# Two sums and two low halves of every moving side on GpSimd in place of VectorE

## The chip, the cores and the metric

One core of a Trainium2 chip runs the whole kernel. The metric is the device time of one execution in microseconds (us). The engines are named as in the profile: PE is TensorE (matmuls), DVE is VectorE, ACT is ScalarE, POOL is GpSimd, SP is the engine that issues most of the loads.

## The reference, cut to what matters

Two transformer blocks in fp32 on a sequence of 2048 tokens of width 1024. The first mixes tokens (a pooling, a differential attention and a stick-breaking attention) and ends in a gated feed-forward layer; the second has a modulated norm, a gated MLP over chunks and a retention, an output projection and a gated residual.

```python
def first_block(x, ...):
    h = rmsnorm(x, norm1_g[l]); p = einsum('bsd,de->bse', h, w_in[l])
    ...
    x = x + einsum('bse,ed->bsd', concat([pool, diff, stick]), w_out[l])
    h2 = rmsnorm(x, norm2_g[l])
    gate = jnp.einsum('bsd,df->bsf', h2, w_gate[l])
    up = jnp.einsum('bsd,df->bsf', h2, w_up[l])
    x = x + jnp.einsum('bsf,fd->bsd', jax.nn.silu(gate) * up, w_down[l])
    return rmsnorm(x, final_norm_g)

def hybrid_layer(x, c, ...):           # the second block
    h = rmsnorm_2(x, g_pre) * (1.0 + scale[:, None, :]) + shift[:, None, :]
    proj = jnp.einsum('bsd,de->bse', h, w_in)
    ...
    y = rmsnorm_2(jnp.einsum('bsm,md->bsd', y, w_out), g_post)
    return x + gate[:, None, :] * y
```

The dense products of the feed-forward layer (width 2816) and of the second block's projections are the ones that this case is about.

## The kernel before, in words

**Products.** Every fp32 matmul is made of three products of halves: an operand `x` is split into a high half, which ScalarE writes (`split`, the copy L133), and a low half, the difference, which VectorE writes (L134); high·high, high·low and low·high are added up in PSUM. The dense layers add a scheme with seven products in place of eight on 2x2 blocks (`seven`, products L1025). Its left operands (stationary, tiles `l` and the sums `sf` of L1001) change with every step; its right operands (moving, tiles `r`) stay for a whole group of steps, and are built by `moving`.

**A moving side.** It has seven parts, named 11, t1, t2, t3, 21, 22 and t4, each with one buffer of its own: the blocks 11, 21 and 22 themselves and four sums: t1 = 11 − 12 (L949), t2 and t3 = 22 less what stands in the buffers (L980), and t4 = 21 less t2's source (L949 again, with the argument `a`; below it is called the fourth sum). The sources are loaded in pieces of 128x1024 into the pool `stg` of five buffers (L937, issued by SP); block 22 is loaded twice, once for L980 and once for its own split. Each part has two pieces, so a part takes two high halves on ScalarE and two low halves on VectorE. A step's products use the parts in the order 11, t1, t2, t3, 21, 22, t4.

**Where they are built.** Eight times a moving side is replaced while products go on: twice for the hidden layer (`hidden_moving`), three times for the way down (`down_moving`, groups of 6, 8 and 8 blocks of the hidden width; in the first group the second piece is 128x512), and three times in the second block (`second_moving`). A part can be written as soon as the last product with the old part is through, so at such a seam the building runs between the last steps of the old side and the first of the new one. The parts of a ninth moving side, at the very start (`first=True`), are built in another order.

**Order.** The program is written as above, and a scheduler with priorities (`high_priority`) sets the order on each engine; each engine then works strictly in its order. Other names: `wk` and `acc` are work tiles and PSUM banks of the products, with the additions L1042, L1044, L1132, L1137 and L1199 that read PSUM on VectorE; L1031 copies the first product; L1129 and L1189 are output transfers that GpSimd issues; L1403 to L1406 are the rotary embedding of the second block, of which L1404 runs on GpSimd or VectorE; L1624 to L1628 the group norm of the retention, with small operations L180 and L182 on GpSimd; L814 an addition of the attention stage on GpSimd.

Of the kernel before, what the change touches and what calls it, by code (L numbers as in the profile page):

```python
# [9 lines left out]
F32 = mybir.dt.float32  # L10
# [3 lines left out]
ALU = mybir.AluOpType  # L14
# [96 lines left out]
class Body:  # L111
# [15 lines left out]
        return self.tc.high_priority(self.pri[kind])  # L127


    def split(self, hi, lo, src):  # L130

        nc = self.nc
        nc.scalar.activation(hi, src, AF.Copy)  # L133
        nc.vector.tensor_tensor(out=lo, in0=src, in1=hi.bitcast(F32), op=ALU.subtract)  # L134

    def wgroup(self, w, k0, nk, c0, ncols):

# [804 lines left out]
    def moving(self, get, nk, first=False):  # L942

        nc = self.nc
        pieces = [(c, min(2, nk - c)) for c in range(0, nk, 2)]

        def less(out, x, y, engine=nc.vector):
            for (c, n), o, u, v in zip(pieces, out, x, y):
                engine.tensor_tensor(out=o[:, :n], in0=u[:, :n], in1=v[:, :n], op=ALU.subtract)  # L949

        def part(name, src):
            t = self.t(self.rp[name], [P, 2, 4, TB], "r", F32R, align=512)
            for (c, n), u in zip(pieces, src):
                self.split(t[:, 0, c:c + n], t[:, 1, c:c + n], u[:, :n])
            return t
        r = {}
        if first:
            r11, r21 = get(0, 0), get(1, 0)
            r["11"] = part("11", r11)
            r["21"] = part("21", r21)  # L960
            r12, r22 = get(0, 1), get(1, 1)
            r["22"] = part("22", r22)
            less(r11, r12, r11)
            r["t1"] = part("t1", r11)
            less(r11, r22, r11)
            r["t2"] = part("t2", r11)
            less(r12, r22, r12)
            r["t3"] = part("t3", r12)
            less(r11, r21, r11)
            r["t4"] = part("t4", r11)  # L970
            return r
        a = get(0, 0)
        r["11"] = part("11", a)
        b = get(0, 1)
        less(a, b, a)
        r["t1"] = part("t1", a)
        for p in range(len(pieces)):
            (c, n), u = pieces[p], get(1, 1, p)[0]
            for o in (a[p], b[p]):
                nc.vector.tensor_tensor(out=o[:, :n], in0=u[:, :n], in1=o[:, :n], op=ALU.subtract)  # L980
        r["t2"] = part("t2", a)
        r["t3"] = part("t3", b)
        r21 = get(1, 0)
        r["21"] = part("21", r21)
        less(a, r21, a)
        r["22"] = part("22", get(1, 1))
        r["t4"] = part("t4", a)
        return r

# [717 lines left out]
```

## Time and profile before

| what | value |
|---|---|
| median of 3 runs | 3583.6 us (3579.54 to 3586.99) |
| profiled execution, its own time | 3589.32 us |
| its span | 3587.6 us |
| PE busy | 3373.3 us, 94% |
| DVE busy | 2485.1 us, 69% |
| ACT busy | 1638.3 us, 46% |
| POOL busy | 932.3 us, 26% |
| products L1025 | 8400 matmuls, 1962.9 us busy, 66.6 us idle before them |

Busy shares are means over the whole span, whose stages differ. The profiled execution is one of several; the span is what the trace covers, and the execution's own time is 1.7 us more.

### The profile page before, as it was taken

The page shows a single profiled execution, that of the slowest core. Times are in us where ns is not written, and L with a number is a line of the kernel's source. Part 1 is how long each engine was busy: PE and PEld are TensorE (multiplying, and loading weights), DVE is VectorE, ACT ScalarE, POOL GpSimd, SP SyncE. Part 2 cuts the span into 40 slices and gives each one's busy share as a digit, 9 for nine tenths or more (in the row PEclk, how much of TensorE's full clock was granted, in tenths as well). Part 3 has the DMA queues.
Part 4 walks back from the last instruction along what each step waited for, and adds up shares of the span by engine and source line. Part 5 has one row for each costly group of instructions (what it writes and reads, how often), then busy time and mean ns, then how long its engine had stood idle before and what let it go on. Part 6 is the DMA issues. An engine that isn't in the chain of part 4 may idle for free. (4 is left out here: it accounts for less than half of the span.)

```text
span 3587.6 us, 47292 instructions
## 1 busy us (share of the span) xinstructions
PE 3373.3 (94%) x16504; PEld 2790.7 (78%) x16504; DVE 2485.1 (69%) x4265; ACT 1638.3 (46%) x3160; POOL 932.3 (26%) x1328
## 2 busy tenths in 40 slices
PE   7989989998879999999999999989999999999989
PEld 5777868886667877888878888778777878788867
DVE  8566674768888857666696667676759887433586
ACT  5347574647676644333343334333556544222243
POOL 3222243314652111111000000211233343333222
PEclk9999999999989999999999999999999999999999
DMA  5367655555533544333263233765786632422353
GB/s 171 123 201 239 182 155 183 172 162 164 173 110 108 159 138 145 116 106 106 85 217 124 91 122 97 154 156 113 170 211 205 206 112 96 146 86 89 112 177 133
DMA packets 458158, 521.51 MB, mean 145 GB/s; under 512 B 43088, under 2 KB 326400, under 8 KB 457920
## 3 DMA queue, kind: packets, MB, share of 16 engines
q1 hardware_dynamic: 401536, 358.26, 33.6%
q0 software_dynamic: 56384, 160.24, 15.0%
q8 instruction: 130, 2.13, 0.2%
q14 instruction: 108, 0.88, 0.1%
HBM read 360.55 MB, written 157.84 MB: 144 GB/s over the span
## 5 line engine op out<-in xcount | busy, mean ns | idle before, releaser
L1025 PE MATMUL acc<-r,l 128*128 128x512 f32 x8400 | 1962.9, 394 | 66.6 <-ACT r L133 20.4
L1025 PEld LDWEIGHTS acc<-r,l 128*128 128x128 f32 x8400 | 1585.4, 190 | 417.3 <-ACT r L133 29.3
L133 ACT ACTIVATE l<-sf 128x512 fp32r<-128x512 f32 (+1 forms) x408 | 251.9, 623 | 550.6 <-PE acc L1025 352.0
L133 ACT ACTIVATE l<-raw 128x512 fp32r<-128x512 f32 (+1 forms) x306 | 189.8, 622 | 423.2 <-PE acc L1025 406.5
L134 DVE TENSOR_TENSOR l<-sf,l 128x512 fp32r<-128x512 f32 (+1 forms) x408 | 280.7, 689 | 73.0 <-ACT l L133 70.8
L679 PE MATMUL s<-k,q 128*128 128x512 f32 (+2 forms) x960 | 272.1, 393 | 30.9 <-DMA q<-qkd 7.1
L134 DVE TENSOR_TENSOR l<-raw,l 128x512 fp32r<-128x512 f32 (+1 forms) x306 | 208.8, 687 | 125.9 <-ACT l L133 125.6
L679 PEld LDWEIGHTS s<-k,q 128*128 128x128 f32 x960 | 166.3, 197 | 68.4 <-DVE s L710 14.6
L1129 POOL DMA_DIRECT2D act<-wk x88 | 48.7, 553 | 621.8 <-DVE wk L1128 613.9
L806 DVE TENSOR_TENSOR_SCAN s<-s,one 128x512 f32<-128x512 f32 (+3 forms) x160 | 187.4, 1203 | 22.3 <-ACT s L802 15.7
L1001 DVE TENSOR_TENSOR sf<-raw 128x512 f32<-128x512 f32 (+1 forms) x102 | 74.5, 731 | 177.2 <-DMA raw<-act 89.3
L717 ACT ACTIVATE s<-s,mx 128x128 f32<-128x128 f32 (+15 forms) x128 | 154.3, 1206 | 84.7 <-DVE mx L713 82.5
L133 ACT ACTIVATE r<-stg 128x1024 fp32r<-128x1024 f32 (+1 forms) x120 | 120.5, 1028 | 123.7 <-PE d L162 23.6
L1189 POOL DMA_DIRECT2D x<-wk x96 | 83.3, 886 | 321.3 <-DVE wk L1199 225.0
L160 PE MATMUL d<-ws,h 128*128 128x512 f32 (+1 forms) x384 | 153.4, 402 | 0.7 <-DVE h L213 0.7
L738 PE MATMUL o<-v,pT 128*128 128x128 f32 x1088 | 149.2, 277 | 4.9 <-ACT pT L746 4.5
L738 PEld LDWEIGHTS o<-v,pT 128*128 128x128 f32 x1088 | 140.7, 192 | 15.5 <-ACT pT L746 8.2
L162 PE MATMUL d<-ws,h 128*128 128x512 f32 (+1 forms) x384 | 146.9, 385 | 0.0
L161 PE MATMUL d<-ws,h 128*128 128x512 f32 (+1 forms) x384 | 146.7, 384 | 0.0
L814 POOL TENSOR_TENSOR s<-s,s 128x1024 f32<-128x1024 f32 x48 | 123.8, 2579 | 73.1 <-DVE s L806 47.1
L134 DVE TENSOR_TENSOR r<-stg,r 128x1024 fp32r<-128x1024 f32 (+1 forms) x120 | 140.6, 1188 | 2.9 <-ACT r L133 2.8
L134 DVE TENSOR_TENSOR ws<-raw,ws 128x1024 fp32r<-128x1024 f32 x72 | 95.4, 1328 | 53.4 <-ACT ws L133 52.8
(322 smaller groups left out, 5777.5 us busy)
## 6 DMA issues: line engine op xcount, KB each, us to landing
raw<-in_w_in_dram SPq DMA_DIRECT2D x72, 512.0 KB, 4.6
k<-qkd SPq DMA_DIRECT2D x120, 256.0 KB, 4.3
q<-qkd SPq DMA_DIRECT2D x96, 256.0 KB, 4.6
x<-wk POOLq DMA_DIRECT2D x96, 256.0 KB, 5.7
raw<-in_w_gate_dram SPq DMA_DIRECT2D x44, 512.0 KB, 4.0
raw<-in_w_up_dram SPq DMA_DIRECT2D x44, 512.0 KB, 3.9
act<-wk POOLq DMA_DIRECT2D x88, 256.0 KB, 3.0
v<-vd SPq DMA_DIRECT2D x80, 256.0 KB, 3.2
```

The source lines that it names most:

```text
L133: nc.scalar.activation(hi, src, AF.Copy)
L134: nc.vector.tensor_tensor(out=lo, in0=src, in1=hi.bitcast(F32), op=ALU.subtract)
L160: self.nc.tensor.matmul(ps, st(0), mv(0), start=i == 0, stop=False)
L161: self.nc.tensor.matmul(ps, st(0), mv(1), start=False, stop=False)
L162: self.nc.tensor.matmul(ps, st(1), mv(0), start=False, stop=i == n - 1)
L679: nc.tensor.matmul(ps[:, :w], q[:, hl, c * P:(c + 1) * P], kt[:, o:o + w], start=hl == 0, stop=hl == 1 and not extra)
L717: nc.scalar.activation(e[:, :nk], e[:, :nk], AF.Exp, scale=-1.0, bias=mx[:, m, np_ - 1:np_], accum_out=s1[:, c, m:m + 1])
L738: nc.tensor.matmul(ops[:, c * P:(c + 1) * P], pT[:, j * P:(j + 1) * P], vs[kt // NT][:, kt % NT], start=kt == 0, stop=kt == nt - 1)
L806: nc.vector.tensor_tensor_scan(out=omb[:, c, :w][:, ::-1], data0=omb[:, c, :w][:, ::-1], data1=self.one.to_broadcast([P, w]), initial=1.0 ...
L814: nc.gpsimd.tensor_tensor(out=beta[:, two], in0=beta[:, two], in1=omb[:, two, 1:w + 1], op=ALU.mult)
L1025: nc.tensor.matmul(ps, l[lk][:, a, k], r[rk][:, b, k], start=first and k == 0 and i == 0, stop=k == nk - 1 and i == 2, skip_group_check=no ...
L1189: nc.gpsimd.dma_start(out=self.x1_d[b][row + i * P:row + (i + 1) * P, j * TB:(j + 1) * TB], in_=t, accum_op=ALU.add)
```

## The change

In the eight moving sides that are built while products go on, the fourth sum (both pieces) and the low halves of block 22 (both pieces) are computed by GpSimd in place of VectorE. The operations, their shapes and their operands stay the same.

```diff
-    def split(self, hi, lo, src):
+    def split(self, hi, lo, src, engine=None):
 
         nc = self.nc
         nc.scalar.activation(hi, src, AF.Copy)
-        nc.vector.tensor_tensor(out=lo, in0=src, in1=hi.bitcast(F32), op=ALU.subtract)
+        (engine or nc.vector).tensor_tensor(out=lo, in0=src, in1=hi.bitcast(F32), op=ALU.subtract)
...
-        def part(name, src):
+        def part(name, src, engine=nc.vector):
             t = self.t(self.rp[name], [P, 2, 4, TB], "r", F32R, align=512)
             for (c, n), u in zip(pieces, src):
-                self.split(t[:, 0, c:c + n], t[:, 1, c:c + n], u[:, :n])
+                self.split(t[:, 0, c:c + n], t[:, 1, c:c + n], u[:, :n], engine)
...
         r["21"] = part("21", r21)
-        less(a, r21, a)
-        r["22"] = part("22", get(1, 1))
+        less(a, r21, a, nc.gpsimd)
+        r["22"] = part("22", get(1, 1), nc.gpsimd)
         r["t4"] = part("t4", a)
```

The scheduler sets new orders. At the second seam (from 1786 us, the second half of the tokens in the hidden layer) GpSimd's rows read as follows. The tiles are: stg_16998 and stg_17000 (last number of the name) the two pieces of the fourth sum, stg_17036 and stg_17038 block 21, stg_17047 and stg_17049 block 22, r_17051 part 22.

```order
 L1129 DMA act2_0_99<-wk_3898_16823 128x512
+L949 TENSOR_TENSOR stg_3925_16998<-stg_3935_17036,stg_3925_16998 128x1024
 L1129 DMA act2_0_99<-wk_3924_16979 128x512
+L949 TENSOR_TENSOR stg_3926_17000<-stg_3936_17038,stg_3926_17000 128x1024
+L134 TENSOR_TENSOR r_3940_17051<-stg_3938_17047,r_3940_17051 128x1024
 L1129 DMA act2_0_99<-wk_3922_16963 128x512
+L134 TENSOR_TENSOR r_3940_17051<-stg_3939_17049,r_3940_17051 128x1024
```

The four new rows stand between the issues of three output transfers, which GpSimd did alone here before.

On VectorE at the same place (part t2 is r_17026, t3 r_17031, 21 r_17040, t4 r_17056) the rows before were:

```order
L134 TENSOR_TENSOR r_3933_17026<-stg_3926_17000,r_3933_17026 128x1024
L949 TENSOR_TENSOR stg_3925_16998<-stg_3935_17036,stg_3925_16998 128x1024
L134 TENSOR_TENSOR r_3934_17031<-stg_3929_17009,r_3934_17031 128x1024
L1001 TENSOR_TENSOR sf_3947_17073<-sf_3945_17068,raw2_3942_17061 128x512
L1001 TENSOR_TENSOR sf_3949_17078<-raw2_3942_17061,raw2_3943_17063 128x512
L134 TENSOR_TENSOR r_3937_17040<-stg_3936_17038,r_3937_17040 128x1024
L134 TENSOR_TENSOR l_3946_17070<-sf_3945_17068,l_3946_17070 128x512
L1128 TENSOR_TENSOR wk_3922_16963<-wk_3922_16963,wk_3918_16932 128x512
L949 TENSOR_TENSOR stg_3926_17000<-stg_3936_17038,stg_3926_17000 128x1024
```

In the new order the two rows of L949 are gone from this stretch, and so are part 22's two rows some places later; the rest of it stands in the same order, and t4's first low half has moved up into the place behind it.

On ScalarE at the fourth seam (from 2338 us, the second group of the way down; t3 is r_21337, 21 r_21346, 22 r_21357, t4 r_21362):

```order
 L133 ACTIVATE r_4721_21332<-stg_4714_21306 128x1024
+L133 ACTIVATE r_4729_21362<-stg_4713_21304 128x1024
 L133 ACTIVATE r_4722_21337<-stg_4717_21315 128x1024
-L133 ACTIVATE r_4729_21362<-stg_4713_21304 128x1024
 L133 ACTIVATE r_4725_21346<-stg_4724_21344 128x1024
 L133 ACTIVATE r_4728_21357<-stg_4726_21353 128x1024
+L133 ACTIVATE r_4729_21362<-stg_4714_21306 128x1024
 L133 ACTIVATE l_4736_21381<-sf_4735_21379 128x512
 L133 ACTIVATE r_4728_21357<-stg_4727_21355 128x1024
 L133 ACTIVATE l_4738_21386<-sf_4737_21384 128x512
-L133 ACTIVATE r_4729_21362<-stg_4714_21306 128x1024
```

Both high halves of t4 have moved up, the first ahead of t3's second piece.

## Rows read from the trace of the kernel before

**Rows 1.** Waits of PE over the whole run: us in total, times, longest.

```profile
PE acc L1025 <- ACT r L133: 20.4, 19, 2.3
...
PE acc L1025 <- DVE r L134: 8.3, 10, 1.7
```

**Rows 2.** Windows of eight seams: us, busy PE, PEld, DVE, ACT, POOL, clock, DMA.

```profile
2217.00:2248.00 31.00, 29.96 (x131) 24.16 (x130) 30.92 (x49) 17.89 (x30) 1.66 (x3) 1.00 0.52 157
...
sum 325.00, PE 276.94 PEld 217.06 DVE 314.64 ACT 168.62 POOL 43.97; mean PE 34.62 PEld 27.13 DVE 39.33 ACT 21.08 POOL 5.50
```

**Rows 3.** Lines L949 and L814: duration ns least/median/most, first and last start.

```profile
L949 DVE TENSOR_TENSOR stg<-stg,stg x32: 685/1219/1234, 1303.4 to 3415.3; 128x1024 f32<-128x1024 f32 x30, 128x512 f32<-128x512 f32 x2
...
L814 POOL TENSOR_TENSOR s<-s,s x48: 2162/2282/3187, 501.0 to 1114.7; 128x1024 f32<-128x1024 f32 x48
```

**Rows 4.** Timeline at 2839.5: start us, duration us, engine, line, tiles, shapes.

```profile
2839.82 0.68 DVE L1001 TENSOR_TENSOR sf<-sf,raw 128x512 f32<-128x512 f32 x1
2839.99 1.66 POOL L1404 TENSOR_TENSOR wk<-wk,rot 128x512 f32<-128x512 f32 x1 [6.02 <-DVE wk L1383]
2840.42 1.78 DVE L1001 TENSOR_TENSOR sf<-raw,raw 128x512 f32<-128x512 f32 x1
```

**Rows 5.** Timeline at 2884 to 2899, within S7.

```profile
2886.59 11.37 POOL L1404 TENSOR_TENSOR wk<-wk,rot 128x512 f32<-128x512 f32 x1 [1.63 <-DVE wk L1383]
...
2897.99 0.42 DVE L1405 TENSOR_TENSOR wk<-wk,wk 128x256 f32<-128x256 f32 x1 [1.19 <-POOL wk L1404]
```

**Rows 6.** Timeline of S2, 1805 to 1822: part of DVE and PE.

```profile
1805.80 1.23 DVE L134 TENSOR_TENSOR r<-stg,r 128x1024 fp32r<-128x1024 f32 x1
...
1810.48 1.23 DVE L134 TENSOR_TENSOR r<-stg,r 128x1024 fp32r<-128x1024 f32 x1
...
1811.61 1.23 DVE L949 TENSOR_TENSOR stg<-stg,stg 128x1024 f32<-128x1024 f32 x1
...
1814.03 1.42 PE L1025 MATMUL acc<-r,l 128*128 128x512 f32 x5 [0.72 <-DVE r L134]
...
1815.08 1.23 DVE L134 TENSOR_TENSOR r<-stg,r 128x1024 fp32r<-128x1024 f32 x1
...
1816.37 5.81 PE L1025 MATMUL acc<-r,l 128*128 128x512 f32 x24 [0.92 <-DVE r L134]
```

**Rows 7.** Timelines of S1, S4 and S6: PE where it idled.

```profile
1390.34 1.88 PE L1025 MATMUL acc<-r,l 128*128 128x512 f32 x7 [0.31 <-DVE r L134]
...
2368.32 5.41 PE L1025 MATMUL acc<-r,l 128*128 128x512 f32 x16 [0.52 <-DVE r L134]
...
2714.36 1.43 PE L1025 MATMUL acc<-r,l 128*128 128x512 f32 x5 [0.92 <-DVE r L134]
...
2720.38 1.88 PE L1025 MATMUL acc<-r,l 128*128 128x512 f32 x7 [1.93 <-ACT r L133]
```

**Rows 8.** Timeline of S5, 2522 to 2541; SP's row from its own timeline.

```profile
2524.60 1.23 DVE L134 TENSOR_TENSOR r<-stg,r 128x1024 fp32r<-128x1024 f32 x1 [1.89 <-ACT r L133]
...
2529.62 1.22 DVE L949 TENSOR_TENSOR stg<-stg,stg 128x1024 f32<-128x1024 f32 x1
...
2530.90 1.47 SPq L937 DMA_DIRECT2D stg<-in_w_down_dram  x2
...
2535.95 5.28 PE L1025 MATMUL acc<-r,l 128*128 128x512 f32 x22 [2.28 <-ACT r L133]
```

**Rows 9.** Timeline of S7, 2874 to 2892.

```profile
2880.49 2.35 DVE L980 TENSOR_TENSOR stg<-stg,stg 128x1024 f32<-128x1024 f32 x2
...
2889.30 2.93 PE L1025 MATMUL acc<-r,l 128*128 128x512 f32 x6 [4.64 <-ACT wk L1031]
```

**Rows 10.** Timeline of S8, 3414 to 3430.

```profile
3417.98 1.07 POOL L1624 TENSOR_TENSOR vq<-rn_m,c_ret_qdec 128x4 f32<-128x4 f32 x1 [5.58 <-DVE rn_m L1476]
...
3422.47 1.11 DVE L1628 TENSOR_SCALAR tmp<-tmp,rn_m,vq 128x128 f32<-128x128 f32 x4 [1.20 <-POOL vq L1626]
...
3424.97 5.18 PE L1025 MATMUL acc<-r,l 128*128 128x512 f32 x12 [3.82 <-DVE l L134]
```

## Prediction

> **What bounds the kernel now.** I read the page first: TensorE is busy almost throughout, and the question is where it is not. The view of TensorE's waits [rows 1] names, among others, the two operations that build a moving side: products L1025 waited 20.4 us for the high halves (ScalarE, L133) and 8.3 us for the low halves (VectorE, L134) of tiles `r`. The timeline then puts nearly all of that at eight places, the seams at which the stationary weights change and a new moving side must be built: S1 at 1366–1400 us, S2 1786–1832, S3 2217–2248, S4 2338–2382, S5 2505–2547, S6 2685–2732, S7 2861–2906, S8 3389–3425. The third view, busy time in these windows [rows 2], shows who is short there: VectorE worked 314.64 of 325.00 us, ScalarE 168.62, GpSimd 43.97. TensorE lacks 325.00 − 276.94 = 48 us in them. So VectorE is the bound of the seams, GpSimd looks free, and outside them neither matters. The reader is to see why one would move rows from VectorE to GpSimd, and then ask whether the two can work at the same time.
>
> **The change part by part.** Per seam four instructions go from VectorE to GpSimd: two L949 (the fourth sum, t4's source) and two L134 (low halves of block 22). That is 8 × 4 = 32, of which 30 are 128x1024 and 2 are 128x512; nothing else is added, no bytes and no product.
>
> *What a row costs on each side.* On VectorE a 128x1024 row takes 1.22 us [rows 3], and consecutive rows start about 1.14 us apart (1811.61 less 1810.48 is 1.13, [rows 6]); the 32 rows are about 31 × 1.14 = 35 us of VectorE's time. On GpSimd I find a subtraction or addition of this shape only in the attention stage: L814, 2.16 us at least and 2.28 in the median [rows 3]. I take 2.16, since the least is the one that waited for nobody.
>
> *Whether they overlap.* This decides. In [rows 4] VectorE ran the same L1001 shape twice: 0.68 us, and then 1.78 us for the row that began at 2840.42, when GpSimd's L1404 (from 2839.99 to 2841.65) was running; the second ended 0.55 us after L1404's end, as if it had been held and then done. In [rows 5] it is the other way round: GpSimd's L1404, the same shape that took 1.66, took 11.37 us from 2886.59 while VectorE went from row to row, and it ended at 2897.96, in VectorE's next gap (1.19 us idle, released by that very L1404). So a GpSimd row and a VectorE row with both inputs in SBUF take turns. GpSimd's turn holds VectorE for 2.16 us, and each moved row gives VectorE 1.14 and can take 2.16: a loss of 1.02 rather than a gain of 1.14. Over 32 rows that is about 33 us of VectorE time more in place of 35 less.
>
> The Trainium skill, "SBUF — State Buffer", section "SBUF: two separate sides", states this as a rule: VectorE and GpSimd share a port pair under an exclusive lock, which a VectorE instruction with two SBUF inputs or a GpSimd instruction takes for its whole length, whichever starts first, and the other blocks fully. By that rule moving work between the two gains nothing while both have work; the trace agrees (1.78 beside 0.68, and 11.37 beside 1.66), and shows besides that a dense row of VectorE instructions can keep GpSimd out for 11 us. With the rule the sum is the one worked out below; without it, each engine at its own pace, the 35 us of relief would lead to the third rival's time.
>
> *What of it lies on TensorE's path.* Only rows that TensorE waits for within the seam count; the moved rows themselves are needed late (22 and t4 are the last products of a step), and the 24 matmuls from 1816.37 on run in one piece [rows 6], so what VectorE is relieved of there is worth nothing.
>
> S2, worked in full [rows 6]. TensorE idles 0.72 before 1814.03 and 0.92 before 1816.37, both times for a low half; the second of these halves, begun on VectorE at 1815.08, ended at 1816.31, 0.06 before TensorE went on: no slack. In the new order both sums stand on GpSimd. The first has its operands at 1807.03 (VectorE's split of the tile at 1805.80 is through), before these rows; the second has them when the row of 1810.48 is through. Each can hold VectorE for 2.16, and one removed L949 (1811.61) gives back 1.14. With both holds the row of 1815.08 is 2 × 2.16 − 1.14 = 3.2 us late, with one 1.0; TensorE follows it. I take 2.6, nearer to the upper end, as both sums are ready while VectorE is full.
>
> S1, S4, S6 have the same build, and again rows that end when TensorE waits for them [rows 7]: 0.31, 0.52 and 0.92 us idle behind DVE r L134. Bounds as in S2, 1.0 to 3.2; middle 2.1 each, 6.3 together. In S4 the order of ScalarE moves too: t4's first high half, which waits for GpSimd's sum, now stands ahead of t3's second.
>
> S5 may gain. There the sum L949 at 2529.62 sets free the staging buffer into which the first piece of block 22 is loaded: the load is issued on SP's queue at 2530.90, and TensorE idles 2.28 until 2535.95 for the high half that ScalarE makes of it [rows 8]. VectorE had a gap of 1.89 us before 2524.60, with the sum's operands there at its end; GpSimd can run it then, and the load goes out about 4 us earlier. At best that takes away 2.28; at worst the same holds as elsewhere cost 1.0. I take −1.5.
>
> S7: the pair L980 at 2880.49 reads the buffer into which the next piece is loaded, so the load goes out behind it, and TensorE idles 4.64 until 2889.30 at the end of that chain [rows 9]. The first sum's operand is ready at 2880.5, so GpSimd can step in between the two: 0 to 2.16, I take +1.5. S8: TensorE idles 3.82 behind a chain of small GpSimd instructions, L1624 at 3417.98 to the multiply L1628 at 3422.47 that waits for it [rows 10]; the last moved row stands within this chain in GpSimd's order: 0 to 2.2, I take +1.1. In S3 TensorE works 29.96 of 31.00 us [rows 2], so little waits: 0 to 1.0, I take +0.3.
>
> Sum: 2.6 + 6.3 − 1.5 + 1.5 + 1.1 + 0.3 = **+10.3 us**. The bounds together: 1.0 + 3.0 − 2.3 + 0 + 0 + 0 = +1.7, and 3.2 + 9.6 + 1.0 + 2.2 + 2.2 + 1.0 = +19.2. The profiled execution took 3589.3 us, 5.7 above the median of 3583.6, so I expect about 3599.6 for a profiled execution like it and **3594** for the median.
>
> **The rivals.**
> *Shut out.* GpSimd does not step in but waits, as in [rows 5], some 10 us behind VectorE's rows. Then VectorE is not held at first, but t4's sum is late; ScalarE and VectorE, which work in order, then stand before t4's halves with other splits behind them. A seam in which that happens loses 5 to 10 us in place of 1 to 3. For it: the 11.37. Against: VectorE has gaps as soon as it lacks an input, and L1404 of [rows 4] did get in at once. In two to four seams it makes +15 to +30: **3599 to 3614**, middle 3606.
>
> *Nothing to see.* The holds fall into time that VectorE has to spare, for it is given 1.14 us a row back too; the late rows are made up before TensorE reads them. This needs most of the terms at their lower bound: −3 to +6, **3581 to 3590**. Against it stand the rows without slack at S2 and [rows 7].
>
> *Faster.* If GpSimd works beside VectorE without holding it, or gets its turns only in VectorE's gaps, the earlier loads and lighter VectorE are all gain: 2.28 in S5, the same kind of wait in S6, where a L949 also stands before a load (1.93 idle at 2720.38, [rows 7]), the waits for low halves 1.14 in S2, 0.52 in S4, 0.31 in S1, and 1.1 in S8, where one row less stands before the chain: 7.3 us, **3576**. It decides from the point where a seam's four rows cost VectorE less than the 4.6 us that they give it: fewer than about two held turns a seam. [Rows 4] speak against it.
>
> **How the numbers follow.** The forecast (held turns, some seams slower by 1 to 3 us) has 0.52, shut out 0.14, nothing to see 0.22, faster 0.12. About 0.2%, 7.2 us, is what a measurement of this kernel tells from no change. Slower by more than that, above 3590.8: four fifths of the forecast's own cases (0.42), all of the first rival (0.14), a little of the second (0.04): 0.60. Faster, below 3576.4: some two thirds of the third: 0.09. Same: the rest, 0.31. The likeliest case's own range is 3585 to 3603. For 8 in 10 I go up into the first rival, to 3610, and down to 3580, through most of the second.
>
> **What would show it.** Right: moved rows on GpSimd of 2.2 us and more in the seams, VectorE rows of 3.3 us beside them (1.22 + 2.16 less what had passed), TensorE's wait for `DVE r L134` in S2, S4 and S6 up by 1 to 3 us each from 8.3 in all [rows 1], its wait at 2535.95 in S5 shorter. Wrong: VectorE rows that stay at 1.22 beside GpSimd's (no turns), or GpSimd rows of 10 us (the first rival), or a TensorE whose waits in the seams are those of before. What would make the number wrong though the turns are right: the scheduler's new order on ScalarE, whose effect I have put at nothing but for S4.

## The result, and the profile after

The changed kernel takes 3613.2 us (median of 4 runs, 3608.1 to 3617.3) where the kernel before takes 3583.4 (4 runs): 29.8 us more, ratio 1.0083 (95% interval 1.0065 to 1.0100). Slower was forecast, and the reason given for it is what the trace shows; but the sum of +10 was a third of it, and 3613 lies above the range. The profiled execution took 3608.1 us, its span 3606.1. The spans of the two profiled executions differ by 18.5 us only: the one before took 8.5 us longer to reach S1, a stretch that the change does not touch, so the two traces are compared seam by seam here.

The moved rows themselves and two of the groups beside them, by line (duration ns least/median/most, first and last start; here as in the later fences of this view):

```profile
L949 POOL TENSOR_TENSOR stg<-stg,stg x16: 1736/3290/7330, 1367.0 to 3426.3; 128x1024 f32<-128x1024 f32 x15, 128x512 f32<-128x512 f32 x1
...
L134 POOL TENSOR_TENSOR r<-stg,r x16: 1612/2855/3403, 1382.8 to 3436.8; 128x1024 fp32r<-128x1024 f32 x15, 128x512 fp32r<-128x512 f32 x1
...
L134 DVE TENSOR_TENSOR r<-stg,r x104: 678/1214/3421, 18.7 to 3435.6; 128x1024 fp32r<-128x1024 f32 x98, 128x512 fp32r<-128x512 f32 x6
...
L1001 DVE TENSOR_TENSOR sf<-sf,raw x102: 549/683/2892, 15.6 to 3563.7; 128x512 f32<-128x512 f32 x94, 128x384 f32<-128x384 f32 x8
```

A row that took 1.22 us on VectorE [rows 3] takes 3.29 and 2.86 us on GpSimd in the median, up to 7.33. And VectorE's rows of the same lines, which before never exceeded 1.24 (`r<-stg,r`) and 0.71 (`sf<-sf,raw`), now reach 3.42 and 2.89, which is the usual row and 2.2 us on top. Counted over the trace from 1340 us on, VectorE has 50 additions and subtractions that are over 0.3 us longer than the usual row of their size, 73.6 us too long together; before there were 19 with 16.2. So 31 rows more are held, for 57 us: 29 of the 32 moved rows run beside such a long row.

TensorE's waits over the whole run, the answer to [rows 1]:

```profile
PE acc L1025 <- ACT r L133: 22.0, 16, 2.6
...
PE acc L1025 <- DVE r L134: 14.4, 11, 3.3
...
PE acc L1025 <- DVE wk L1042: 6.2, 3, 3.8
...
PE acc L1025 <- POOL r L134: 3.5, 2, 3.1
```

The wait for low halves from VectorE rose from 8.3 to 14.4; new are waits for VectorE's PSUM additions (L1042, 0.3 us before), and for GpSimd's own rows.

S2 in the timeline, beside [rows 6]:

```profile
1801.79 5.05 POOL L949 TENSOR_TENSOR stg<-stg,stg 128x1024 f32<-128x1024 f32 x1 [20.13 <-DVE r L134]
...
1805.12 3.94 DVE L134 TENSOR_TENSOR r<-stg,r 128x1024 fp32r<-128x1024 f32 x2
...
1807.97 2.58 PE L1025 MATMUL acc<-r,l 128*128 128x512 f32 x10 [0.85 <-DVE r L134]
1808.06 3.24 POOL L949 TENSOR_TENSOR stg<-stg,stg 128x1024 f32<-128x1024 f32 x1 [0.72 <-issue]
1808.98 2.87 DVE L1001 TENSOR_TENSOR sf<-sf,raw 128x512 f32<-128x512 f32 x1
...
1811.41 1.06 ACT L133 ACTIVATE r<-stg 128x1024 fp32r<-128x1024 f32 x1 [3.38 <-DMA stg<-hT]
...
1812.52 11.21 PE L1025 MATMUL acc<-r,l 128*128 128x512 f32 x41 [1.97 <-ACT r L133]
1812.55 3.28 POOL L134 TENSOR_TENSOR r<-stg,r 128x1024 fp32r<-128x1024 f32 x1 [1.25 <-ACT r L133]
...
1813.51 2.87 DVE L134 TENSOR_TENSOR l<-sf,l 128x512 fp32r<-128x512 f32 x1
...
1825.17 1.20 PE L1025 MATMUL acc<-r,l 128*128 128x512 f32 x4 [1.45 <-DVE wk L1044]
```

The reader sees the turns. The first sum waits 2.9 of its 5.05 us behind VectorE's rows and then holds the one of 1805.12 (the two rows take 3.94 in place of 2.35). The second holds L1001 at 1808.98 for 2.2 us, and the halves of part 22, one of which is shown, hold rows of the stationary side (1813.51). The last line is where these come back: TensorE waits 1.45 us for an addition (L1044) that stands behind the held rows on VectorE; before, the same matmul had no wait. The longest wait, 1.97 us at 1812.52, has another path: ScalarE's split at 1811.41 needs a load that SP issued at 1806.86, when the first sum, after its 2.9 us of waiting, had set the buffer free (SP had waited 3.4 us for it).

S1 shows the other face:

```profile
1375.48 7.33 POOL L949 TENSOR_TENSOR stg<-stg,stg 128x1024 f32<-128x1024 f32 x1 [4.83 <-DMA stg<-hT]
...
1382.84 1.06 ACT L133 ACTIVATE r<-stg 128x1024 fp32r<-128x1024 f32 x1 [6.29 <-POOL stg L949]
...
1385.17 2.11 PE L1025 MATMUL acc<-r,l 128*128 128x512 f32 x8 [3.06 <-POOL r L134]
```

Here GpSimd was shut out for five microseconds behind VectorE's rows. ScalarE stood 6.29 us before t4's high half, which needs this sum, with other splits behind it, and TensorE then waited 3.06 us for part 22's low half, which stands behind the sum on GpSimd. In the whole run ScalarE waited so in five places, 16.2 us.

Busy time in the eight seams, cut a little wider and at the same matmuls in both traces (sums over the eight; columns as in [rows 2]), before and after:

```profile
sum 437.00, PE 387.17 PEld 307.66 DVE 394.96 ACT 211.76 POOL 76.29; mean PE 48.40 PEld 38.46 DVE 49.37 ACT 26.47 POOL 9.54
```

```profile
sum 466.21, PE 394.60 PEld 312.11 DVE 418.88 ACT 214.11 POOL 169.46; mean PE 49.32 PEld 39.01 DVE 52.36 ACT 26.76 POOL 21.18
```

The seams are 29.2 us longer, and every single one is (2.2 to 5.0 us; the most in S8, 50.00 to 55.01). VectorE is busy 24 us more with 32 rows less. TensorE idles 21.8 us more (71.6 against 49.8) and is busy 7.4 us more with the same matmuls. In the second term is the clock, as the windows of S2 behind its idle time of 1.97 us show:

```profile
1808.00:1810.00 2.00, 2.00 (x9) 1.59 (x10) 2.00 (x2) 0.04 (x1) 1.94 (x1) 1.00 0.81 208
...
1814.00:1816.00 2.00, 2.00 (x6) 1.58 (x5) 2.00 (x1) 1.40 (x2) 1.83 (x1) 0.50 0.63 158
...
1818.00:1820.00 2.00, 2.00 (x11) 1.64 (x10) 2.00 (x3) 0.08 (x1) 2.00 (x1) 1.00 0.67 190
```

The granted clock fell to 0.50 (1.2 GHz in place of 2.4) after the idle stretch and was back by 1818; before, S2 ran at 1.00 throughout. How far such windows can be trusted: e9 and e11 below have the very order of the kernel before on every engine, and their seams, cut in the same way, sum to 444.9 and 441.6, with TensorE busy for 392.1 and 390.7. So up to 8 of the 29 us, and 3.5 to 5 of the 7.4, lie within what one execution differs from the next (S5 took 58.98 in e11 and S6 64.14 in e9, against 59.68 and 63.40 with the change; S8 took 50.17 and 49.72); of the idle time, 53 and 51 us there, some 19 to 22 are the change's.

### The profile page after: what moved, and what is told of

The parts are those of the page before. It is cut to its first block, busy times and chain, and to the rows that moved or that the text cites. A ratio compares the mean times of both kernels' runs of the same rounds, so it can differ in the third digit from the quotient of the medians.

```text
span 3606.1 us, 47329 instructions
## 1 busy us (share of the span) xinstructions
PE 3379.6 (94%) x16504; PEld 2793.4 (77%) x16504; DVE 2505.8 (69%) x4233; ACT 1638.1 (45%) x3160; POOL 1028.9 (29%) x1360
## 4 chain that ended last, share of the span: by engine, by line
PE 59%; DVE 14%; issue 5%; DMA 5%; POOL 4%; ACT 3%; SPq 0%; DVEq 0%; POOLq 0%; ACTq 0%
PE acc L1025 33%; PE d L160 5%; PE d L162 5%; PE d L161 5%; PE o L738 3%; PE s L679 3%; DVE s L806 2%; DVE r L134 2%; DVE l L134 2%; DVE sf L1001 1%; PE tp L744 1%; DMA raw<-act 1%; DVE pT L134 1%; DMA raw<-h 1%; PE tp L833 1%
## 5 line engine op out<-in xcount | busy, mean ns | idle before, releaser
L134 DVE TENSOR_TENSOR l<-sf,l 128x512 fp32r<-128x512 f32 (+1 forms) x408 | 298.6, 734 | 76.5 <-ACT l L133 74.2
L134 DVE TENSOR_TENSOR l<-raw,l 128x512 fp32r<-128x512 f32 (+1 forms) x306 | 206.3, 678 | 121.5 <-ACT l L133 121.3
L806 DVE TENSOR_TENSOR_SCAN s<-s,one 128x512 f32<-128x512 f32 (+3 forms) x160 | 187.5, 1203 | 22.2 <-ACT s L802 15.8
L1001 DVE TENSOR_TENSOR sf<-raw 128x512 f32<-128x512 f32 (+1 forms) x102 | 70.1, 687 | 175.4 <-DMA raw<-act 81.2
L134 DVE TENSOR_TENSOR r<-stg,r 128x1024 fp32r<-128x1024 f32 (+1 forms) x104 | 145.1, 1412 | 7.2 <-ACT r L133 7.2
L814 POOL TENSOR_TENSOR s<-s,s 128x1024 f32<-128x1024 f32 x48 | 123.9, 2581 | 72.2 <-DVE s L806 46.0
L134 DVE TENSOR_TENSOR ws<-raw,ws 128x1024 fp32r<-128x1024 f32 x72 | 94.7, 1318 | 53.5 <-ACT ws L133 53.1
```

Source lines behind the costliest of these rows:

```text
L134: (engine or nc.vector).tensor_tensor(out=lo, in0=src, in1=hi.bitcast(F32), op=ALU.subtract)
L806: nc.vector.tensor_tensor_scan(out=omb[:, c, :w][:, ::-1], data0=omb[:, c, :w][:, ::-1], data1=self.one.to_broadcast([P, w]), initial=1.0 ...
L814: nc.gpsimd.tensor_tensor(out=beta[:, two], in0=beta[:, two], in1=omb[:, two, 1:w + 1], op=ALU.mult)
L1001: engine.tensor_tensor(out=t, in0=x, in1=y, op=op)
```

## The experiments

Each is timed in five rounds or more beside the kernel before; the differences are of medians.

**e1, e2: half of the change each.**

```diff
-        less(a, r21, a)
+        less(a, r21, a, nc.gpsimd)        # e1
-        r["22"] = part("22", get(1, 1))
+        r["22"] = part("22", get(1, 1), nc.gpsimd)        # e2
```

> Only the fourth sum (16 rows) on GpSimd, the low halves of 22 back on VectorE. Theory T (turns: each moved row takes about 2.2 us from VectorE and gives 1.14 back, and a seam is as long as VectorE's work in it): half of the change's cost, +13 to +17 us on the kernel before. Theory L (lateness: what costs is that ScalarE and TensorE wait for the moved row's own result, the sum above all): +20 to +28, most of the change's +30. The prediction's own sum, in which the rows of 22 counted only in S8: +9.

> Only the low halves of block 22 (16 rows) on GpSimd, the fourth sum back on VectorE. Theory T: the other half, +13 to +17 us. Theory L: +2 to +8, since part 22 is needed late. The prediction's own sum, which gave these rows nothing but in S8: +1.

e1: +14.8 us, ratio 1.0045 (1.0032 to 1.0057). e2: +16.9 us, 1.0048 (1.0035 to 1.0061). Held rows: 15 and 15 more than before, 27 and 28 us. The two halves add up to the whole, and the low halves of 22, to which the prediction gave 1 us, cost as much as the sums. In S5 of e1 the predicted gain can be seen by itself: the first sum begins in VectorE's gap, and runs 1.4 us beyond its end.

```profile
2531.54 2.37 POOL L949 TENSOR_TENSOR stg<-stg,stg 128x1024 f32<-128x1024 f32 x1 [5.33 <-DMA stg<-in_w_down_dram]
2532.48 2.51 DVE L134 TENSOR_TENSOR r<-stg,r 128x1024 fp32r<-128x1024 f32 x1 [3.15 <-ACT r L133]
...
2538.98 2.58 POOL L949 TENSOR_TENSOR stg<-stg,stg 128x1024 f32<-128x1024 f32 x1 [2.21 <-DMA stg<-in_w_down_dram]
2539.22 2.88 DVE L1001 TENSOR_TENSOR sf<-raw,raw 128x512 f32<-128x512 f32 x1
...
2539.88 4.60 PE L1025 MATMUL acc<-r,l 128*128 128x512 f32 x19 [0.84 <-ACT r L133]
...
2545.04 1.20 PE L1025 MATMUL acc<-r,l 128*128 128x512 f32 x4 [0.56 <-DVE r L134]
```

The idle 2.28 of [rows 8] is gone: its matmul is the seventh of the 19 from 2539.88. But both sums hold a row (2.51 and 2.88), a low half is waited for 0.56 later on, and this seam came out as long as in the execution before. In e2 TensorE waits for the moved rows themselves, the low halves of part 22, 2.9 of it in S1:

```profile
PE acc L1025 <- POOL r L134: 6.8, 4, 2.9
```

**e3: the hold without the relief.**

```diff
+        def shadow(t4, t):
+            for c, n in pieces:
+                u = t[:, 0, c:c + n].bitcast(F32)
+                nc.gpsimd.tensor_tensor(out=t4[:, 1, c:c + n], in0=u, in1=u, op=ALU.subtract)
         r["21"] = part("21", r21)
+        shadow(t4, r["21"])        # the same behind part 22
```

> The kernel before, with VectorE doing all its rows, and in each seam four more GpSimd subtractions of the same shape with two inputs from SBUF, started by the high halves of parts 21 and 22; nobody uses what they write (it is overwritten by t4's low half). Theory T: all of the hold and none of the relief, 32 x 2.2 us = 70 at most; +35 to +65 us, VectorE rows of 2.8 to 3.4 us beside each. Theory L: nothing is late, so at most +7.

+35.4 us, 1.0105 (1.0090 to 1.0121), at the lower end of what was expected; 25 more rows held, 40 us. Nobody uses what these rows, the shadows, write; only t4's low half, which overwrites it, must wait for them, and VectorE did so once, for 3.0 us. So lateness of a result can be little of it.

**e4, e6: fills in place of the shadows.**

```diff
-                nc.gpsimd.tensor_tensor(out=t4[:, 1, c:c + n], in0=u, in1=u, op=ALU.subtract)
+                nc.gpsimd.memset(t4[:, 1, c:c + n].bitcast(F32), 0.0)
+                nc.gpsimd.memset(t4[:, 1, c:c + n].bitcast(F32), 1.0)
```

This is e6, which also drops the argument `t`; e4 keeps a subtraction of 128x1 ahead of each two fills.

> As e3, but in place of each subtraction a tiny one of 128x1 and two fills of 128x1024 that read nothing. If turns are taken only with a GpSimd row that reads SBUF beside a VectorE row with two inputs from it: -2 to +6 us, and VectorE rows stay at 1.2 us beside the fills. If any GpSimd row holds VectorE: like e3 by its own duration, +20 or more. Theory L: 0 to +5.

> As e4 without the tiny subtractions: eight fills of 128x1024 a seam on GpSimd, waiting only for t4's buffer, so t4's low half waits for no late fill. If only GpSimd rows that read SBUF take turns with VectorE: within 3 us of the kernel before, and no VectorE row longer than 1.3 us beside a fill. If every GpSimd row does: 8 x 8 x 0.95 = 61 us of turns, so +15 to +40.

Both missed: e4 +14.4 (1.0044, 1.0032 to 1.0057), e6 +13.7 (1.0040, 1.0026 to 1.0053). That no row is held came true: in e6 the low halves on VectorE keep to 1.23 us, and no more rows are long than before (17 against 19).

```profile
L134 DVE TENSOR_TENSOR r<-stg,r x120: 678/1215/1226, 19.4 to 3425.8; 128x1024 fp32r<-128x1024 f32 x113, 128x512 fp32r<-128x512 f32 x7
```

In e4 the tiny subtraction itself was shut out, and t4's low half waited for the fill behind it (18.9 us in 9 places); its line:

```profile
L959 POOL TENSOR_TENSOR r<-r x32: 184/825/12340, 1369.0 to 3429.0; 128x1 fp32r<-128x1 f32 x32
```

An instruction of 0.18 us took up to 12.34. e6 has no such wait and costs the same. The orders of e3, e4 and e6 differ from that of before on all engines. e3 and e4 have the same order on TensorE, ScalarE and SP and all but seven rows on VectorE, so e4 is the control for e3: the holds of e3 are worth about 35.4 − 14.4 = 21 us, or more if e4's late low halves cost it time. e6 has an order of its own (some 160 of TensorE's matmuls stand elsewhere than in e3), and gives 22. The 14 of e6 are not explained; the new order is a candidate, since in its trace the stretch from S7 to S8, in which no fill runs, took 477.4 us against 469.0 before (470.7 and 468.6 in e9 and e11).

**e9, e11: two edits that came out as no change.** e9 asks for t4's buffer as early as e3 to e6 do; e11 gives the sum on VectorE a higher priority.

```diff
+        t4 = self.t(self.rp["t4"], [P, 2, 4, TB], "r", F32R, align=512)        # e9
+        with self.tc.high_priority(100):        # e11
+            less(a, r21, a)
```

> Control for e3, e4 and e6: the kernel before with t4's buffer asked for early, right after part 21, as those three do, and nothing on GpSimd. If the early buffer and the scheduler's other order cost the 14 us of e4 and e6: +9 to +17 us, and then the turns alone are e3 less this, about 22. If the fills of e6 cost them after all: within 3 us of the kernel before.

> The kernel before with the fourth sum at higher priority, still on VectorE, so that it goes out earlier and sets free the buffer into which part 22 is loaded: the gain that the prediction looked for in S5 and S6, without GpSimd. If the loads behind the sum bound the seams: -3 to -8 us. If the sum then only pushes back another row that TensorE needs: -2 to +6.

The scheduler put out the order of the kernel before for both, so e11 tells nothing of an earlier sum, and both serve as repeats: +1.1 us (1.0001, 0.9991 to 1.0010) and −1.8 (0.9999, 0.9989 to 1.0010).

**e5, e10: the relief.** e5 leaves the 16 sums and the 16 low halves of part 22 out; e10 has the changed kernel with two fills for each subtraction, and leaves out the same.

```diff
-        less(a, r21, a)
-        r["22"] = part("22", get(1, 1))
+        r["22"] = part("22", get(1, 1), False)        # e5: no low half
-                engine.tensor_tensor(out=o[:, :n], in0=u[:, :n], in1=v[:, :n], op=ALU.subtract)
+                nc.gpsimd.memset(o[:, :n], 0.0)        # e10, where engine is nc.gpsimd
+                nc.gpsimd.memset(o[:, :n], 1.0)
```

> The 32 rows are left out altogether (t4 is split without its last subtraction, and products with part 22 read its high half in place of the low one): VectorE is relieved and nobody holds it. Theory T: the change is the sum of the hold (e3: +38 in the seams) and this relief, so -6 to -10 us. If the relief of 35 us of VectorE's time in the seams came through whole, -25 to -35. Theory L with no relief to be had: -3 to 0.

> The change with two fills of GpSimd (0.96 us each, reading nothing) in place of each of its 32 subtractions: the sums and part 22's low halves are left out, but t4's high half still waits for GpSimd and the rows are off VectorE. Theory T (turns make the cost): none, so about like e5, -8 to +4 us. Theory L (t4 waits for another engine, and the scheduler's new order on ScalarE and TensorE): +10 to +25. A GpSimd that disturbs VectorE whatever it does: +10 or more, with long VectorE rows beside the fills.

e5: −3.8 us (0.9990, 0.9980 to 0.9999). e10: −10.4 (0.9980, 0.9970 to 0.9989). Without subtractions on GpSimd the same relief and the same engines, in another order, make the kernel faster, not slower; the 35 us of VectorE's time bring 4 to 10. What TensorE then waits for is what it waited for before, here in e5:

```profile
PE acc L1029 <- ACT r L133: 20.2, 17, 2.3
...
PE acc L1029 <- ACT r L957: 5.8, 5, 2.0
...
PE acc L1029 <- DVE r L134: 5.4, 5, 2.0
```

26.0 us for ScalarE's high halves (20.4 in [rows 1]); only the 5.4 are VectorE's (8.3 before). ScalarE itself stood before these splits for loads (57 us from 1340 us on) more than for VectorE's sums (31).

**e13, e14: the hold with little of the wait.** e5 with e3's subtractions (e13), and with e6's fills (e14); the same parts are left out as in e5.

```diff
         r["21"] = part("21", r21)
+        shadow(t4, r["21"])
         r["22"] = part("22", get(1, 1), False)
+        shadow(t4, r["22"])
```

> e5 (the 32 rows off VectorE, sums and low halves left out) with the four GpSimd subtractions a seam of e3 beside it: VectorE is relieved and held as in the change, but ScalarE and TensorE wait for no result of GpSimd and no buffer is set free by one. If the turns alone make the change's +30: +24 to +34 over the kernel before. If half of it is the wait of ScalarE for GpSimd's sum (16.2 us in the trace of the change): +8 to +20. If the turns cost nothing without that wait: -4 to +4.

> The control for e13, and for the +14 of e6: the same with the fills of e6, which read nothing, in place of the subtractions. If fills cost nothing and e6's +14 is the scheduler's order in that kernel: within 5 us of e5 and e10, -10 to +2. If fills on GpSimd cost by themselves: +6 to +14.

e13: +13.2 us (1.0036, 1.0024 to 1.0049). e14: −10.0 (0.9975, 0.9964 to 0.9985). The two differ in what GpSimd runs, and in the order that the scheduler makes of it: 23 us for 25 more held rows and 37 us, of the size that e3 and e4 gave for the hold; against e5 it is 17. t4's low half, which overwrites what the subtractions write, made VectorE wait 6.0 us for them in two places (2.1 for a fill in e14), so a little lateness is left. The fills cost nothing here.

**e7: 48 rows.** The change and part 21's low halves too.

```diff
-        r["21"] = part("21", r21)
+        r["21"] = part("21", r21, nc.gpsimd)
```

> The change and the low halves of part 21 as well on GpSimd: 48 rows. Theory T: half as much again as the change, +40 to +52 us. If the cost of the change saturates (VectorE has slack once 32 rows are off it): +25 to +33. If late rows pile up on GpSimd, each 2.2 us and more in a chain that part 21 needs soon: over +55.

+62.0 us, 1.0170 (1.0156 to 1.0184): 16 rows more cost 32 us, twice as much a row as in the change. 42 rows more than before are held, for 84 us, and TensorE waits for GpSimd directly, where part 21 is needed soon:

```profile
PE acc L1025 <- POOL r L134: 13.3, 6, 8.5
```

**e8: the other direction.** The 8 rows L1404 that GpSimd did go to VectorE.

```diff
-        (nc.gpsimd if in_sbuf else nc.vector).tensor_tensor(out=s_, in0=x, in1=tab[1], op=ALU.mult)
+        nc.vector.tensor_tensor(out=s_, in0=x, in1=tab[1], op=ALU.mult)
```

> The opposite direction at one place: the 8 rows of the rotary embedding that GpSimd did (L1404, one of them within S7) go to VectorE. Theory T: 8 x (1.7 held less 0.6 worked) = 9 us of VectorE's time back, most of it where TensorE does not wait for VectorE: -3 to 0 us. Theory L: 0.

−2.6 us, 0.9994 (0.9984 to 1.0004): not told apart from no change.

**e12: the fourth sum by a transfer.** What stands in t4 is then not the fourth sum, so only the time is read.

```diff
-        less(a, r21, a)
+        for c, t in zip(range(0, nk, 2), a):
+            nc.gpsimd.dma_start(out=t[:, :n], in_=load(1, 0, c, n), accum_op=ALU.add)
```

> The fourth sum without VectorE and without a GpSimd subtraction: t2's source is kept with the other sign (L1042 then subtracts), and block 21 is added to it in SBUF by a transfer that GpSimd issues and that loads the block a second time. Theory T: 16 rows off VectorE and no turns; e10 gave -10 for 32 rows, so -3 to -8 us, with VectorE rows of 1.2 us beside the issues. If the added 8 MB of loads or the length of such a transfer delay t4 or the other loads: 0 to +10. If issuing on GpSimd holds VectorE as a subtraction does: +5 to +15.

+18.2 us, 1.0047 (1.0032 to 1.0062). No more rows are held than before (20 against 19), and 16 rows are off VectorE, so turns do not make this: the result is late. Its line:

```profile
L936 POOL DMA_DIRECT2D stg<-in_w_down_dram x6: 934/1213/1237, 2236.8 to 2542.4; - x6
...
  ACT r L133: 46.6, 14
DMA to landing us min/median/max: 6.5/9.0/11.4
```

The transfer lands after 9.0 us in the median (4.4 to 5.4 for plain loads into these buffers in the kernel before), and ScalarE, which takes its rows in order, waits 46.6 us in 14 places for it with splits behind that TensorE needs.

## Why the prediction was right and wrong

**The mechanism was right, its place too narrow, and two terms were missing.** That the two engines take turns, that a turn is 2.2 us, that the moved rows would read 2.2 us and more (1.6 and 1.7 for the two of half the size) and VectorE's up to 3.4: all as written. The price of 1.02 us a moved row makes 33 us of VectorE's time for 32 rows, and the kernel lost 30; that the two agree is in part luck, for 35 us of relief brought 4 to 10. The step that failed is the next one: "Only rows that TensorE waits for within the seam count; the moved rows themselves are needed late […] so what VectorE is relieved of there is worth nothing". By it the rows of part 22 were given 1 us in all, in S8; e2 measured 17. They were not needed late everywhere: TensorE waited for them directly, 6.8 us in four places (e2). And in S2 they hold rows of the next step's stationary side, 1813.51 above, and by these the addition that TensorE waits for at 1825 (1.30 us in e2 as well). A row behind which TensorE runs on "in one piece" has slack only as long as nothing holds the rows after it.

**The sums** were given some 9 us and cost 15 (e1). S1, S2, S4, S6 at 1.0 to 3.2 and S7 at 0 to 2.2 left out what comes after the hold. The path was not the predicted one either: the waits for `DVE r L134` were to rise by 1 to 3 us each in S2, S4 and S6, and went from 1.6 to 0.9, 2.9 to 2.2 and 1.4 to 3.3. In S2 and S4 the waits for ScalarE's high halves rose instead (0.3 to 2.3 and 5.0 to 8.0). In S2 the scheduler's new order on TensorE has a share: by the two orders, the first product with part 22 now stands ahead of those with 21's second low half, for which the prediction let TensorE wait, and the 1.97 us are for 22's high half. The prediction put the new order at nothing but on ScalarE in S4; some 200 of TensorE's matmuls have changed places.

**S8** was given 1.1, at most 2.2, and is the seam that lost most, 5.0. The wait of 3.82 in [rows 10] became 8.70. Where TensorE takes up the new side, before, and the rows after:

```profile
3419.07 2.07 PE L1025 MATMUL acc<-r,l 128*128 128x512 f32 x4 [11.79 <-ACT l L133]
```

```profile
3426.92 2.72 DVE L1001 TENSOR_TENSOR sf<-sf,raw 128x512 f32<-128x512 f32 x1
...
3429.68 2.77 POOL L134 TENSOR_TENSOR r<-stg,r 128x1024 fp32r<-128x1024 f32 x1 [0.59 <-ACT r L133]
3430.16 3.37 DVE L134 TENSOR_TENSOR r<-stg,r 128x1024 fp32r<-128x1024 f32 x1
...
3432.61 2.08 PE L1025 MATMUL acc<-r,l 128*128 128x512 f32 x4 [12.19 <-ACT l L133]
...
3435.80 1.09 POOL L1624 TENSOR_TENSOR vq<-rn_m,c_ret_qdec 128x4 f32<-128x4 f32 x1 [3.35 <-DVE rn_m L1476]
3436.84 2.33 POOL L134 TENSOR_TENSOR r<-stg,r 128x1024 fp32r<-128x1024 f32 x1
...
3440.88 1.11 DVE L1628 TENSOR_SCALAR tmp<-tmp,rn_m,vq 128x128 f32<-128x128 f32 x4 [4.06 <-POOL vq L1626]
...
3443.38 5.36 PE L1025 MATMUL acc<-r,l 128*128 128x512 f32 x12 [8.70 <-DVE l L134]
```

The moved row within the chain (3436.84), which the prediction priced, lengthens it from L1624 to L1628 by 0.6 us only. The chain begins 4.3 us later: 3.2 us behind TensorE's start at 3432.61, where before it began 1.1 ahead of it (3417.98 and 3419.07). What it needs stands behind VectorE's held rows, and in the new order behind more of VectorE's rows than before; how these two share the 4.3 is open. The same wait was 8.2 us in e3 and 7.3 in e13, and was not there in e5 and e14.

**S5** was to gain 1.5. The mechanism is there (the 2.28 are gone in e1, and with the change too), but holds in the same seam take it back: with the change TensorE waits 3.32 for a low half some matmuls later, and the seam was 3.7 us longer than in the execution before, 0.7 to 2.0 longer than in e9 and e11.

**The rival "shut out" was not a rival.** It was priced as what happens in place of the hold; both happen in one seam, the second sum of S1 waiting five microseconds and its successors holding VectorE after that. Its 3599 to 3614 holds the measured time, which is no proof of it. (Of the 11.37 us in [rows 5], 1.66 are the row's own, so GpSimd was kept out for 9.7, not 11.) L949 rows of 5.05 to 7.33 us stand in S1, S2, S3 and S7, the number of seams that it named.

**The clock** was left out: with the two repeats beside it, 2.5 to 4 us of slower matmuls in the seams are the change's (394.6 against 392.1 and 390.7).

**VectorE as the bound of the seams** was half true, and this was the first step. It was busy 314.64 of 325.00 us [rows 2], but taking 35 us of work off it brings 4 to 10 us (e5, e10, e14), near the third rival's 7.3. The row that matters is the wait, and [rows 1] had it: 20.4 us for ScalarE's splits, 8.3 for VectorE's. Of these 28.7 us, 22.2 fall into the seams, which is less than half of the 48 that TensorE lacked there. An engine may be busy through a stage with work that the end of the stage does not need.

**The sum as it now stands.** Relief −10 (e14, e10; e5 has −4); the hold +23 (e13 less e14; e3 less e4 gives 21, e13 less e5 17); the rest of the way to +30, 17 us, lies between e13 and the change. Part of that is more hold, since the change holds rows for 57 us and e13 for 37: at e13's rate, 23/37 = 0.62, the 57 us cost 36, which would leave some 4 for the wait for GpSimd's late results. Part is this wait: ScalarE's 16.2 us, and e12, in which no more rows are held, cost 18 with a late sum. Part can be the scheduler's order, which differs between e13 and the change on every engine. How these 17 us divide is not settled, nor what e6's 14 are.

The Trainium skill, "SBUF — State Buffer", section "SBUF: two separate sides", has the lock as an exclusive one for a whole instruction, and has a VectorE instruction with two SBUF inputs meet it only against a GpSimd instruction that reads SBUF; e6, e10 and e14 agree on the last part: beside fills, which read nothing, VectorE's low halves stay at 1.23 us.

## What to carry to other kernels

Before work is moved from VectorE to GpSimd, look for what a GpSimd row does to the VectorE rows beside it; if they take turns, compare the GpSimd row's length with the VectorE time that it gives back (2.2 against 1.14 here), and count every moved row, not only those that a wait stands behind. Read which wait ends last before calling an engine the bound: VectorE was 97% busy in the seams, and a tenth of its work taken away gave 0.1 to 0.3% of the kernel. Try a fill on GpSimd in place of the real operation, and a shadow that nobody reads beside it: the first tells what the relief is worth, the second what the hold costs. Compare kernels of one order, as e3 and e4, for the scheduler's order changes with every such edit.

## What was not expected of the hardware

A GpSimd subtraction of 128x1, 0.18 us by itself, took up to 12.34 us beside a dense VectorE (e4; 0.83 in the median of 32): being short did not always help to get a turn. And in S2 the granted clock fell to 0.50 for 3.4 us, from 1813.4 to 1816.8, behind an idle stretch of 1.97 us in which TensorE had waited for one split.
